# Giving the mixers of the second block instruction regions of their own

## The chip, the cores and the metric

The kernel runs on one core of a Trainium2 chip. The metric is device time in microseconds (us) of one execution. TensorE (PE) multiplies matrices, VectorE (DVE) and ScalarE (ACT) do element work, GpSimd (POOL) does some of it too, and SyncE (SP) starts transfers. Each engine runs its own list of instructions strictly in order; an instruction that waits for another engine holds up everything behind it in its list.

## The reference, cut to what matters

The program is a chain: a first transformer block with attention and a state-space part, a product-key expert layer ("Peer"), and a second block of two layers over 512 tokens of width 1024. A layer of the second block is

```
x = x + 0.5 * swiglu(rmsnorm(x, ffn1_norm), ffn1_gate, ffn1_up, ffn1_down)
z = rmsnorm(x, mix_norm) @ w_in
(aq, ak, av, iq, ik, iw, bq, bk, bv, bg, br, cu, dcq, dckv, dkpe) = split(z)
y_a = dsa_mixer(...)    # attention over the 256 or fewer keys that an index score picks
y_b = gla_mixer(...)    # gated linear attention in chunks of 64 tokens
y_c = conv_mixer(...)   # gate, 31-tap depthwise convolution, rmsnorm, silu
y_d = mla_mixer(...)    # latent attention with rope
x = x + concat([y_a, y_b, y_c, y_d]) @ w_out
x = x + 0.5 * swiglu(rmsnorm(x, ffn2_norm), ffn2_gate, ffn2_up, ffn2_down)
```

All of it is float32. The two layers have the same shapes.

## The kernel before, in words

The residual x stays in SBUF as hT: 8 chunks of 128 features by 512 tokens. Every large matrix product is taken as three matmuls (mm3, lines 209 to 211): weights and activations are split into a rounded high part and a low rest (wh, wl; xh, xl), and the products wh·xh, wh·xl and wl·xh are summed in PSUM. Weights arrive by SP transfers; `lw` copies the high part on ACT (line 1027) and subtracts it on DVE or POOL (line 1028).

The layer function (line 981) calls `ffn`, `mixer`, `ffn`. The `ffn` ends with 8 additions to hT on DVE (line 1067). Both begin with `scaled`, which makes xh on ACT (line 995) and xl on DVE (line 996) chunk by chunk, and with `rows_rstd` (squares on ACT at 1006, their sum on POOL at 1008).

The `mixer` writes its steps in an order laid down by hand (ORDER, line 830). The steps that matter here:

- "hp" and "conv" project the convolution's input (line 1558 is its first DVE instruction) and run 62 DVE instructions over 512 tokens (1571, 1573).
- "index" and "topk1" to "topk3" score keys and keep 256 of them: 16 rounds of a maximum and a replacement on DVE (1282, 1283), closed by line 1284, for 256, 384 and 512 columns.
- "mla0" to "mla3" are softmax blocks of the latent attention, 128 query rows and 4 heads each, over 128 to 512 keys: scores on PE (1432), scaled on ACT (1435) and on DVE (1436), then `softmax_pv`: maxima (DVE, 1220), exponentials (ACT, 1223), one half of the division on ACT and one on DVE (1230), transposes on PE (1233), copies (ACT, 1235) and products with the values (PE, 1240).
- "dsa0" to "dsa3" are the softmax blocks over the picked keys. They need the mask of their topk: bias and mask are added on DVE (1323, 1325), scores on PE (1328) are added to them on DVE (1329), then `softmax_pv`.
- "gla" and "conv_norm" need 1/sqrt of a mean square, taken as Ln (line 216) and Exp (217) on ACT; "silu" applies Silu on ACT (1150) to the gate tiles rg and the convolution's cv, and afterwards asks for the table of Ln and Exp again (1334). ACT holds one set of function tables at a time, and a change of set is an instruction of its own, ACT_TABLE_LOAD.
- "y4", "y2", "y6" split the results into high and low (194 on ACT, 195 on DVE).

Last comes the output projection "wo": 192 matmuls in two halves of 96 (WOP, YORD), the first over the parts of conv, gla and mla, the second over the rest, each added to hT on DVE (1212).

The text order is not the order of execution. A scheduler puts each engine's instructions into a list of its own. The first block stands in a `tc.block(name="first", schedule_with_timeline_sim=True)`; everything behind it, Peer, the four ffn and the two mixers, is one region, so an instruction of an ffn may stand between those of a mixer.

Of the kernel before, what the change touches and what calls it, by code (L numbers as in the profile page):

```python
# [919 lines left out]
class Block2:  # L920
# [60 lines left out]
    def layer(self, l, x):  # L981
        self.vec = self.vec2[:, l]
        self.ffn(l, 0, x)
        if l == 0:
            self.constants()
        self.mixer(l, x)
        self.ffn(l, 1, x)

    def scaled(self, x, g):
# [988 lines left out]
```

## Time and profile before

| what | us |
|---|---|
| runs, median (lowest to highest of 3) | 3770.8 (3761.55 to 3776.63) |
| the profiled execution | 3765.66 |
| its span, first to last instruction | 3763.8 |
| PE busy | 3593.1 (95% of the span) |
| DVE busy | 2592.4 (69%) |
| ACT busy | 1412.5 (38%) |
| POOL busy | 1087.1 (29%) |
| mean granted TensorE clock | 0.978 of full speed |

Busy shares are means over stages that differ, so the two mixers are looked at by themselves below. The profile shows them, in time from the span's start, at about 2028 to 2350 us and 3075 to 3400 us. Matmul ends are modelled: one 512-column mm3 matmul is shown as 0.39 us long, but starts follow one another closer than that.

### The profile page before, as it was taken

The numbers are of one execution on the slowest core, as the hardware profiler recorded it, in microseconds if no ns is written. First come the engines' busy times: TensorE is split into PE (matmuls) and PEld (weight loads), VectorE is DVE, ScalarE is ACT, GpSimd is POOL, SyncE is SP. The second block draws the span as 40 slices with busy tenths as digits, with TensorE's granted clock in tenths as the row PEclk, the third lists the DMA queues.
The fourth block names the chain that finished last, engine by engine and source line by source line (L and its number), as shares of the span: only waits on it lengthen the run. The fifth ranks groups of instructions, "written<-read, shape, count | busy, mean of one in ns | idle before, by whom it ended". The sixth has DMA issues, their size and how long they took to land. (4 is left out here: it accounts for less than half of the span.)

```text
span 3763.8 us, 46084 instructions
## 1 busy us (share of the span) xinstructions
PE 3593.1 (95%) x17229; PEld 2972.0 (79%) x17229; DVE 2592.4 (69%) x4504; ACT 1412.5 (38%) x2405; POOL 1087.1 (29%) x685
## 2 busy tenths in 40 slices
PE   7798979889999999999999899999999998999999
PEld 6656878878889988888887667888888875668887
DVE  9668999788888889854445987444444459975443
ACT  3253259423333333342223446322322234453222
POOL 4424767445555555530002222000100012210000
PEclk8899989999999999999999999999999999999999
DMA  4212225888888888833223111323332321112233
GB/s 119 78 40 94 76 91 224 284 304 295 286 307 292 301 291 297 301 111 95 93 98 94 64 46 56 96 95 95 96 95 95 98 93 54 46 45 95 95 96 101
DMA packets 181520, 529.88 MB, mean 141 GB/s; under 512 B 22256, under 2 KB 73008, under 8 KB 163120
## 3 DMA queue, kind: packets, MB, share of 16 engines
q1 hardware_dynamic: 157504, 388.64, 31.0%
q0 software_dynamic: 19392, 136.06, 9.8%
q10 hardware_dynamic: 4400, 2.24, 0.3%
q8 instruction: 136, 2.23, 0.2%
q14 instruction: 88, 0.72, 0.1%
HBM read 495.52 MB, written 30.18 MB: 140 GB/s over the span
## 5 line engine op out<-in xcount | busy, mean ns | idle before, releaser
L1027 ACT ACTIVATE wh<-wr 128x1024 fp32r<-128x1024 f32 (+1 forms) x334 | 347.4, 1040 | 1029.8 <-PE ps L210 766.0
L210 PE MATMUL ps<-x,wh 128*128 128x512 f32 x1408 | 548.8, 390 | 2.1 <-DVE x L996 2.0
L209 PE MATMUL ps<-x,wh 128*128 128x512 f32 x1408 | 549.1, 390 | 0.0
L211 PE MATMUL ps<-x,wl 128*128 128x512 f32 x1408 | 547.9, 389 | 0.0
L1028 DVE TENSOR_TENSOR wl<-wr,wh 128x1024 fp32r<-128x1024 f32 (+1 forms) x288 | 344.4, 1196 | 78.0 <-ACT wh L1027 71.1
L1008 POOL TENSOR_TENSOR s<-s,s 128x512 f32<-128x512 f32 x42 | 67.0, 1596 | 1125.2 <-ACT s L1006 1113.9
L1841 POOL TENSOR_TENSOR vl<-vr,vh 128x1024 fp32r<-128x1024 f32 x128 | 325.4, 2543 | 183.3 <-ACT vh L1840 178.2
L211 PE MATMUL S<-x,wl 128*128 128x384 f32 x1024 | 349.7, 341 | 8.1 <-POOL wl L1802 8.1
L209 PE MATMUL S<-x,wh 128*128 128x384 f32 x1024 | 349.4, 341 | 0.0
L210 PE MATMUL S<-x,wh 128*128 128x384 f32 x1024 | 348.6, 340 | 0.0
L1850 PE MATMUL V<-vl,ah 128*128 128x512 f32 x768 | 302.7, 394 | 12.0 <-POOL vl L1841 12.0
L210 PEld LDWEIGHTS ps<-x,wh 128*128 128x128 f32 x1408 | 264.3, 188 | 61.4 <-DVE x L996 5.9
L1850 PE MATMUL V<-vh,ah 128*128 128x512 f32 x768 | 300.7, 393 | 10.1 <-ACT vh L1840 10.1
L209 PEld LDWEIGHTS ps<-x,wh 128*128 128x128 f32 x1408 | 264.2, 188 | 55.8 <-issue 1.0
L211 PEld LDWEIGHTS ps<-x,wl 128*128 128x128 f32 x1408 | 264.3, 188 | 54.7
L1850 PE MATMUL V<-vh,al 128*128 128x512 f32 x768 | 302.5, 394 | 1.3 <-DVE al L195 1.3
L211 PE MATMUL ps<-ml,wl 128*128 128x512 f32 x704 | 278.1, 395 | 0.0
L209 PE MATMUL ps<-ml,wh 128*128 128x512 f32 x704 | 278.0, 395 | 0.0
L1914 POOL DMA_INDIRECT rows<-in_uv_dram,gidx x128 | 188.1, 1470 | 260.9 <-DVE acc L1923 230.9
L1055 DVE TENSOR_TENSOR s<-ps,rs 128x512 f32<-128x512 f32 x88 | 60.8, 691 | 278.8 <-PE ps L211 278.8
L1067 DVE SCALAR_TENSOR_TENSOR hT<-ps,hT 128x512 f32<-128x512 f32 x96 | 66.3, 691 | 270.7 <-PE ps L211 270.7
L1802 DVE TENSOR_TENSOR wl<-wr,wh 128x1024 fp32r<-128x1024 f32 x100 | 186.9, 1869 | 63.8 <-ACT wh L1800 63.7
(582 smaller groups left out, 7936.7 us busy)
## 6 DMA issues: line engine op xcount, KB each, us to landing
wr<-in_f_gu_dram SPq DMA_DIRECT2D x176, 512.0 KB, 3.7
wr<-in_ut_dram SPq DMA_DIRECT2D x128, 512.0 KB, 5.3
vr<-in_uv_dram SPq DMA_DIRECT2D x128, 512.0 KB, 4.8
wr<-in_f_dn_dram SPq DMA_DIRECT2D x64, 448.0 KB, 3.3
gates<-gst SPq DMA_DIRECT2D x12, 2048.0 KB, 6.8
gt<-gates SPq DMA_DIRECT2D x32, 768.0 KB, 7.3
wr<-in_w_dram SPq DMA_DIRECT2D x46, 512.0 KB, 3.4
wr<-in_f_dn_dram SPq DMA_DIRECT2D x32, 512.0 KB, 3.6
```

The lines of the kernel that those rows point to most:

```text
L209: mm(out, wh, xh, start=start, stop=False)
L210: mm(out, wh, xl, start=False, stop=False)
L211: mm(out, wl, xh, start=False, stop=stop)
L1008: nc.gpsimd.tensor_tensor(sq, acc, sq, op=OP.add)
L1027: nc.scalar.activation(hi, raw, AF.Copy)
L1028: (eng or nc.vector).tensor_tensor(lo, raw, hi.bitcast(F32), op=OP.subtract)
L1055: V.tensor_mul(u, ps[1], r)
L1067: V.scalar_tensor_tensor(x[:, m], ps, 0.5, x[:, m], op0=OP.mult, op1=OP.add)
L1802: e.tensor_tensor(ul, raw, uh.bitcast(F32), op=OP.subtract)
L1841: nc.gpsimd.tensor_tensor(vl, raw, vh.bitcast(F32), op=OP.subtract)
L1850: nc.tensor.matmul(ps[k], x[:, ts], y[:, cs], start=b == 0 and n == 0, stop=b == P - 1 and n == 2)
L1914: nc.gpsimd.indirect_dma_start(r, None, self.A["uv"], bass.IndirectOffsetOnAxis(ap=self.gi[:, s:s + 1], axis=0))
```

## The change

```diff
@@ Block2.layer
         if l == 0:
             self.constants()
-        self.mixer(l, x)
+        with self.tc.block(name=f"mixer{l}", schedule_with_timeline_sim=True):
+            self.mixer(l, x)
         self.ffn(l, 1, x)
```

Each mixer becomes a region of its own, and the scheduler weighs the order inside it by simulating a timeline. The instructions of the program are now: first block; Peer and the first ffn; mixer 0; two ffn; mixer 1; the last ffn. At an edge stands one branch per engine; no engine waits for another there, but no instruction crosses the edge. All lines behind 985 have a number higher by one in the changed kernel (1212 is 1213 there). On PE, DVE, POOL and SP the instructions are the same but for four branches each; on ACT there are also 14 more ACT_TABLE_LOAD, 7 in each mixer.

**ACT, mixer 0, near the last topk.** Before, the last rstd (convn) stands ahead of the Silu of the gate (rg), with one table load for all Silus:

```order
L242 ACTIVATE r_18788<-cv_17835 128x512
L216 ACTIVATE r_18791<-convn_18784,epsc 128x512
L217 ACTIVATE r_18791<-r_18791 128x512
L1223 ACTIVATE sm_18656,st_18676<-sm_18656,st_18676 128x384
L1223 ACTIVATE sm_18657,st_18676<-sm_18657,st_18676 128x384
L1223 ACTIVATE sm_18658,st_18676<-sm_18658,st_18676 128x384
L1223 ACTIVATE sm_18659,st_18676<-sm_18659,st_18676 128x384
L1150 ACT_TABLE_LOAD
L1150 ACTIVATE rg_18830<-rg_18830 128x512
```

Now, with the gate's Silu already done above these rows:

```order
L216 ACT_TABLE_LOAD
L216 ACTIVATE gl_18249<-gla_18245,epsc 128x512
L217 ACT_TABLE_LOAD
L217 ACTIVATE gl_18249<-gl_18249 128x512
L242 ACTIVATE gl_18272<-gla_18254 128x512
L1436 ACTIVATE sm_18378<-mla_18391,rqd_17795 128x128
L216 ACT_TABLE_LOAD
L216 ACTIVATE gl_18275<-gla_18271,epsc 128x512
L217 ACT_TABLE_LOAD
L217 ACTIVATE gl_18275<-gl_18275 128x512
```

The two rstd of gla (gl) and that of convn now come behind the gate's Silu; each loads a table for Ln and another for Exp, and cv's Silu loads a third kind again.

**DVE, mixer 0, at the end of the last topk** (ds is the index score; sm and sd hold softmax scores; the first row of either piece, 1284 before and 1285 now, closes topk3). Before:

```order
L1284 TENSOR_SCALAR ds_17342<-ds_17342 128x512
L1230 TENSOR_SCALAR sm_18657<-sm_18657,st_18676 128x384
L1230 TENSOR_SCALAR sm_18659<-sm_18659,st_18676 128x384
L1323 TENSOR_TENSOR sd_19060<-bias,ds_17342 128x256
L1325 TENSOR_SCALAR sd_19060<-ds_17342,b_16960 128x256
L1323 TENSOR_TENSOR sd_19061<-bias,ds_17342 128x256
```

Now, 13 rows behind that 1285 (between them stand the last splits of gl and dsa3's eight additions and two of its scores):

```order
L1437 SCALAR_TENSOR_TENSOR sm_18442<-mla_18446,rqd_17795,m_16956 128x128
L1221 TENSOR_REDUCE st_18462<-sm_18442 128x1
L1437 SCALAR_TENSOR_TENSOR sm_18443<-mla_18450,rqd_17795,m_16956 128x128
L1213 TENSOR_TENSOR hT<-hT,wo_19306 128x512
L1221 TENSOR_REDUCE st_18462<-sm_18443 128x1
L1213 TENSOR_TENSOR hT<-hT,wo_19320 128x512
L1330 SCALAR_TENSOR_TENSOR sd_19063<-dsa_19077,rq_18765,sd_19063 128x512
```

Before, the last row of an mla block's division (1230, of mla2) stands at the end of topk3. Now all of mla3 (sm_18442 and on) and then all of mla2 stand behind it, among the additions of wo's first half. On PE, the 96 matmuls of that first half stood among the dsa blocks before; now 89 of them stand ahead of mla3's transposes and 7 behind. The second half ended with 90 matmuls in a row before; now 24 of its matmuls stand at mla2 and the scores of dsa0, 12 at the end of dsa1 and dsa2, and 60 in a row behind all else.

**DVE, mixer 0, at its end.** Before, the last additions to hT alternate with the next ffn's xl (996) and its weights (1028):

```order
L1212 TENSOR_TENSOR hT<-hT,wo_19441 128x512
L996 SCALAR_TENSOR_TENSOR x_19591<-hT,vec_14586,x_19583 128x512
L1212 TENSOR_TENSOR hT<-hT,wo_19455 128x512
L1028 TENSOR_TENSOR wl_19505<-wr_19503,wh_19504 128x1024
L996 SCALAR_TENSOR_TENSOR x_19592<-hT,vec_14586,x_19584 128x512
L1212 TENSOR_TENSOR hT<-hT,wo_19475 128x512
```

Now:

```order
L1213 TENSOR_TENSOR hT<-hT,wo_19490 128x512
L1029 TENSOR_TENSOR wl_19506<-wr_19504,wh_19505 128x1024
L1029 TENSOR_TENSOR wl_19540<-wr_19538,wh_19539 128x1024
L1213 TENSOR_TENSOR hT<-hT,wo_19510 128x512
L1213 TENSOR_TENSOR hT<-hT,wo_19524 128x512
L1213 TENSOR_TENSOR hT<-hT,wo_19544 128x512
L1213 TENSOR_TENSOR hT<-hT,wo_19558 128x512
L986 UNCONDITIONAL_BRANCH
L997 SCALAR_TENSOR_TENSOR x_19592<-hT,vec_14586,x_19584 128x512
L997 SCALAR_TENSOR_TENSOR x_19593<-hT,vec_14586,x_19585 128x512
L997 SCALAR_TENSOR_TENSOR x_19594<-hT,vec_14586,x_19586 128x512
L1029 TENSOR_TENSOR wl_19574<-wr_19572,wh_19573 128x1024
```

The two weight tiles of wo's last four chunks (wl_19506, wl_19540) now stand behind the fourth of the last eight additions, and the next ffn's xl and its first weights (wl_19574) behind the eighth. At the entry the same holds: the mixer's eight 997 rows and its first weights stand behind all eight additions of the ffn.

## Rows read from the trace of the kernel before

**Rows 1.** Busy time of each engine by stretch: inside mixer 0, inside mixer 1, two ffn.

```profile
core 0: us, PE busy (x) PEld busy (x) DVE busy (x) ACT busy (x) POOL busy (x), PEclk, DMA share, GB/s
2070.00:2290.00 220.00, 200.54 (x965) 143.30 (x963) 205.25 (x440) 111.33 (x240) 52.02 (x28) 0.96 0.16 52
3110.00:3330.00 220.00, 196.61 (x929) 140.53 (x930) 206.68 (x431) 109.72 (x235) 50.03 (x21) 0.94 0.15 47
2420.00:3070.00 650.00, 650.00 (x2837) 532.16 (x2836) 284.58 (x335) 191.02 (x231) 19.70 (x12) 1.00 0.30 96
```

**Rows 2.** The same view, mixer 0: head to topk3's end, then three parts of the tail.

```profile
2042.00:2267.00 225.00, 203.41 (x962) 148.02 (x963) 208.14 (x419) 104.07 (x219) 56.16 (x30) 0.96 0.18 57
2267.00:2305.00 38.00, 36.29 (x191) 24.20 (x190) 33.26 (x73) 25.17 (x56) 9.90 (x5) 1.00 0.18 56
2305.00:2326.00 21.00, 21.00 (x117) 14.99 (x118) 13.00 (x31) 12.37 (x35) 0.00 (x0) 1.00 0.12 33
2326.00:2348.00 22.00, 22.00 (x98) 18.21 (x97) 16.90 (x18) 12.80 (x19) 8.62 (x6) 1.00 0.26 90
```

**Rows 3.** DVE's waits in mixer 0's head (us in total, times, longest).

```profile
DVE sm L1436 <- ACT sm L1435: 3.2, 4, 1.2
DVE tr L227 <- PE qkn L1297: 2.8, 1, 2.8
```

**Rows 4.** One line's instructions: topk3's closing DVE row, mixer 0 and 1.

```profile
L1284 DVE TENSOR_SCALAR ds<-ds x1: 428/428/428, 2267.1 to 2267.1; 128x512 f32<-128x512 f32 x1
...
L1284 DVE TENSOR_SCALAR ds<-ds x1: 420/420/420, 3313.7 to 3313.7; 128x512 f32<-128x512 f32 x1
```

**Rows 5.** The additions of wo to hT, mixer 0 and 1 (same view).

```profile
L1212 DVE TENSOR_TENSOR hT<-hT,wo x16: 672/679/689, 2287.3 to 2346.9; 128x512 f32<-128x512 f32 x16
...
L1212 DVE TENSOR_TENSOR hT<-hT,wo x16: 671/687/691, 3343.5 to 3396.9; 128x512 f32<-128x512 f32 x16
```

**Rows 6.** DVE's groups of the softmax blocks, mixer 0 (busy us, mean ns).

```profile
L1436 DVE SCALAR_TENSOR_TENSOR sm<-mla,rqd,m 128x128 f32<-128x128 f32 x16 | 5.3, 345 | 3.3 <-ACT sm L1435 3.2
L1220 DVE TENSOR_REDUCE st<-sm 128x1 f32<-128x512 f32 x4 | 2.5, 676 | 0.0
L1323 DVE TENSOR_TENSOR sd<-bias,ds 128x256 f32<-128x256 f32 x8 | 5.4, 689 | 0.5 <-PE dsa L1233 0.5
L1325 DVE TENSOR_SCALAR sd<-ds,b 128x256 f32<-128x256 f32 x4 | 2.2, 556 | 0.0
L1329 DVE SCALAR_TENSOR_TENSOR sd<-dsa,rq,sd 128x512 f32<-128x512 f32 x4 | 3.0, 738 | 0.0
```

**Rows 7.** ACT's groups, 2200 to 2348 us.

```profile
L1223 ACT ACTIVATE sd<-sd,st 128x512 f32<-128x512 f32 x4 | 2.9, 716 | 0.1
L1235 ACT ACTIVATE pt<-dsa 128x512 f32<-128x512 f32 x4 | 2.4, 597 | 2.4 <-PE dsa L1233 2.4
L1150 ACT ACT_TABLE_LOAD x1 | 1.3, 1283 | 0.0
```

**Rows 8.** Timeline at mixer 0's end: start, us, engine (ps: the next ffn's first product).

```profile
2345.76 0.39 PE L209 MATMUL ps<-x,wh 128*128 128x512 f32 x1
...
2347.45 0.74 DVE L996 SCALAR_TENSOR_TENSOR x<-hT,vec,x 128x512 fp32r<-128x512 f32 x1
...
2348.11 1.21 DVE L1028 TENSOR_TENSOR wl<-wr,wh 128x1024 fp32r<-128x1024 f32 x1
```

**Rows 9.** Timeline in mixer 0: PE idle in brackets, then two matmuls.

```profile
2178.45 1.12 PE L1115 MATMUL vtr<-cst,rg 128*128 128x128 f32 x4 [3.71 <-DVE rg L1086]
...
2180.65 0.63 PE L210 MATMUL win<-x,wh 128*128 128x512 f32 x1
2181.07 0.63 PE L211 MATMUL win<-x,wl 128*128 128x512 f32 x1
```

**Rows 10.** Busy time by stretch, as rows 1: PE's granted clock at two places.

```profile
2086.00:2097.00 11.00, 7.72 (x12) 2.83 (x11) 10.87 (x17) 6.52 (x16) 4.72 (x8) 0.53 0.35 105
...
2178.00:2182.00 4.00, 3.55 (x11) 2.94 (x12) 4.00 (x12) 1.18 (x3) 0.00 (x0) 0.57 0.33 113
```

## The prediction

> **What bounds the kernel now.** I read the stretches first. In the two ffn between the mixers PE is busy for the whole 650 us: 2837 matmuls, one every 0.229 us [rows 1]. A new order cannot shorten that, so only the mixers and their edges count. Inside them PE idles about 20 us in 220, while DVE is busy for 205 to 207 [rows 1]. Then I split mixer 0 at the end of its last topk, because the dsa blocks need the mask that topk3 makes. From the convolution's first DVE row to that point (2042 to 2267, "the head") DVE is busy for 208.1 of 225 us [rows 2]: the head is DVE's, with 16.9 us of idle, pieces of one to three microseconds behind ACT and PE [rows 3]. From there to the last addition into hT ("the tail") PE is busy for 36.3 of 38, 21.0 of 21 and 22.0 of 22 us [rows 2]: the tail is PE's, because wo's matmuls fill the time in which the softmax chains wait for DVE and ACT. It runs from 2267.1 to 2346.9 + 0.7 = 2347.6, or 80.5 us; in mixer 1 from 3313.7 to 3397.6, or 83.9 [rows 4, 5].
>
> **The change part by part.** The work is the same but for the table loads; what moves is order. All terms are for one mixer, in microseconds.
>
> *Tail: +11.5.* Before, mla3 and mla2 ran beside topk on DVE, and only the last transposes of mla2 were left when topk3 ended. Now both stand behind it, and I walk their chain with t = 0 at topk3's end:
> - DVE does two splits of 0.68, dsa3's additions 4 × (0.69 + 0.56), four scores of 0.74, mla3's 4 × (0.345 + 0.676) and three additions of wo of 0.68 [rows 5, 6]: 1.4 + 5.0 + 3.0 + 4.1 + 2.0 = 15.5. Then mla3's maxima are there.
> - PE has 89 matmuls of wo ahead of mla3's transposes, 89 × 0.229 = 20.4 [rows 1]. They start at about 2, and their list waits some 1.5 for DVE in between: t = 24. Two halves, each with transposes, two copies of 0.60 [rows 7], products and 7 wo in all, take about 6: t = 30.
> - mla2 starts there. Its scaling, maximum, four exponentials and division cannot overlap anything of its own; at three quarters of the 512-column durations they take 6.5, and the two halves with wo between them 6: t = 42.5.
> - dsa0 and dsa3 together: the remaining scores and maxima 5.5, exponentials 4 × 0.72 + 4 × 0.4 = 4.5, halves 5.5: t = 58. dsa1 and dsa2: DVE 8, exponentials 4.5, halves 6, less 1.5 that overlaps: t = 75. The 0.4 and the 8 are my estimates by width from rows 6 and 7.
> - 60 matmuls of wo, 60 × 0.229 = 13.7. Their last four chunks wait for weights that DVE now subtracts (1.21 [rows 8]) behind the fourth addition of wo: some 2.3. With the last addition: t = 92.
>
> So 92 against 80.5, where before 90 matmuls in a row could not start earlier because PE had been full; now PE idles in the chains. Bounds: if the chains hid entirely, PE's work alone, 192 × 0.229 = 44 plus the small matmuls of four blocks, some 17, would give 61 (-19). If wo's 60 all ran at the slow step below, 92 + 12 (+23.5).
>
> *Exit: +4.5.* Before, the next ffn's first matmul follows wo at once, at 2345.76, because its xl rows and weights alternate with wo's additions [rows 8]. Now they stand behind the eighth addition: wo's last matmul, then 1.1 to the end of that addition, three xl rows of 0.74, and the weights' subtraction of 1.21 [rows 8], without which the third matmul can't start: 1.1 + 2.2 + 1.2 = 4.5. Bounds 0 (if something still covers it) and 6.5 (a second pair of weights).
>
> *Entry: 0.* The same happens there: PE waits about 4 for xl and weights. But the next bound is DVE, which waits for the row norm; its chain of squares and sums keeps its place, and the projections' matmuls were waiting for it before. Bounds 0 to +3.
>
> *Table loads: +3.* 7 × 1.283 = 9.0 on ACT [rows 7], all near topk3's end, where the two splits of cv stand ahead of topk3's last DVE row and wait for cv's Silu. About 20 of DVE's own topk work lies beside these loads, so most is hidden; 0 to 9, and I take a third. The Trainium skill, "ScalarE: Activation LUTs", section "Table sets: the hidden batching unit", says to group activation calls by set, not by function, and this order breaks its rule: Silu is pulled ahead of two Ln/Exp pairs, then comes back. Its price of about 2.7 us for a switch would make it 18.9 on ACT and the sum some 14 higher for both mixers; the row has 1.283 for the load itself, and I go by the row.
>
> *Head: -6.* With each instruction at the usual duration of its group, the DVE list up to topk3's end sums to 186.7 now and to 189.7 in the old order (rows 2 have 208.1 for the old one, since some rows took longer than usual): the work that moved behind it (mla3, mla2) and the work that moved ahead (gate products, splits) nearly cancel, -3. Of the 16.9 of DVE idle [rows 2] the new order may close some or none: it mixes topk with the other chains earlier. No row tells how much; bounds -16 and 0; as each of the pieces has a chain on ACT or PE behind it [rows 3] that the new order does not shorten, I take -3.
>
> *Sum:* 11.5 + 4.5 + 0 + 3 - 6 = +13 for a mixer, +26 for both. The two mixers have the same pieces, and mixer 1's stretches look alike [rows 1], so I don't treat it apart. The profiled execution took 3765.7 us, so 3791.7 by its own time; it lies 5.1 below the median of the three runs, so against that median I expect 3797.
>
> **The rivals.**
>
> *The clock falls in the tail (slower still).* After an idle of 3.71 us PE's matmuls follow one another at 0.42 to 0.43 us instead of 0.229 [rows 9, 1], and the granted clock is 0.57 there, 0.53 in an earlier stretch of 11 us [rows 10]: the lower level, 1.2 GHz. The new tail has some 30 us in which PE has only short work between waits. If one such stretch of 11 us falls into each of the two dsa stages or the wo behind them, it costs up to 5 each: +10 for a mixer, 3797 + 20 = 3817. The Trainium skill, "TensorE: Matmul & The Clock Gate", Part 1, says that the low clock is the default and that activity releases it; rows 10 fit that. Against this rival: in the tail before, the clock was 1.00, and in the new one wo's 89 and 60 run unbroken.
>
> *The idle closes (faster).* DVE's order is the one thing that the head hangs on. If nearly all of the 16.9 goes, the head gains 3 + 16 = 19, and if ACT's loads stay hidden and the exit costs 4.5, the tail decides: with mla2 overlapping mla3's halves and dsa's additions it may come down to 82, +1.5. Then -13 for a mixer: 3771 - 26 = 3745. It decides where the head's gain exceeds what tail and exit cost, 6 in this case and 16 by my walk. For it speaks that DVE's idle is in many short pieces; against it, that two whole softmax chains stand alone behind topk3.
>
> *Order moves the idle about (no change).* Head -12, tail +8, exit +4: 3771. For it: PE and DVE work are unchanged, and each is over 90% busy in the head.
>
> That the change does nothing is excluded by the order of the instructions.
>
> **How the numbers follow.** I give my forecast 0.45, its own range 3780 to 3815; the falling clock 0.14; no change 0.25; faster 0.16. About 0.5% (19 us) is what a measurement of this kernel can tell from no change: below 3752 is faster, above 3790 slower. Of the forecast three quarters lie above 3790: slower 0.34 + 0.14 + 0.02 from the edge of "no change" = 0.50. Same: 0.11 + 0.23 = 0.34. Faster: 0.16. The range leaves out a tenth at each side: it goes down to 3747, into the faster case, and up to 3828, past the falling clock. Likeliest is the forecast, 3797.
>
> **What would show it.** Right: topk3's end at the same distance behind the convolution's first row, 219 to 228 us; the time from there to the last addition of wo 88 to 96 instead of 80.5; PE idle of several microseconds in that tail, which had almost none; a PE gap of 3 to 6 us between the mixer's last wo matmul and the ffn's first; seven more table loads in each mixer, 1.28 each; the ffn stretches unchanged. Wrong: a tail of 80 or less, which would mean that the chains overlap better than I walked them; a head of under 215, which would mean that the idle was order alone; a Peer or ffn stretch whose length changes, since nothing moves there but at the edges; a clock under 0.9 in the tail, which is the first rival.

## The result and the profile after

The changed kernel takes **3882.3 us** (median of four runs, 3880.22 to 3889.28), against 3772.0 for the kernel before beside it (3761.55 to 3776.63): 1.03 times as long, 95% interval 1.0274 to 1.0325. Slower was right; the size, +110 us, is four times the forecast's +26 and lies outside the range.

The profiled execution took 3889.28 us, 7.0 above its median, and that of before lies 6.4 below its own, so the traces show 123.6 where the medians show 110.3. The page of after, its line of busy times:

```profile
PE 3648.7 (94%) x17229; PEld 3005.6 (77%) x17229; DVE 2611.6 (67%) x4504; ACT 1431.3 (37%) x2419; POOL 1096.9 (28%) x685
```

ACT has 14 instructions more, the table loads. PE is busy 55.6 us longer with the same work; the mean granted clock is 0.961 instead of 0.978.

Where the time went is found by cutting each mixer at five instructions that both traces have: the last addition of the ffn (1067, now 1068), the convolution's first DVE row (1558/1559), topk3's closing row (1284/1285), the last addition of wo (1212/1213), and the next ffn's first product row on DVE. In us, mixer 0 / mixer 1:

| stretch | before | after | difference |
|---|---|---|---|
| entry | 12.9 / 12.4 | 21.3 / 17.7 | +8.4 / +5.3 |
| head | 225.2 / 227.6 | 230.9 / 228.1 | +5.7 / +0.5 |
| tail | 80.0 / 83.5 | 122.8 / 119.2 | **+42.8 / +35.7** |
| exit | 12.1 / 12.1 | 23.2 / 23.2 | +11.1 / +11.1 |
| sum | 330.3 / 335.6 | 398.2 / 388.2 | +67.9 / +52.6 |

The sums give 120.5 of the 123.7 by which the spans differ; the stretches of ffn alone are unchanged. The rest lies ahead of the first ffn (3.4), where the program is the same: over the traces of all runs here that point is reached between 1657.0 and 1665.8 us. So a single execution's whole time says less than its stretches. Two thirds of the 120.5 lie in the tail. Busy times of after, mixer 0: the head; then the tail, cut at the ends of the divisions of mla2, of dsa0 and dsa3, of dsa1 and dsa2, and at the last addition; then the exit (columns as in [rows 1]):

```profile
2053.90:2284.80 230.90, 203.70 (x913) 150.12 (x913) 218.60 (x404) 107.96 (x202) 62.01 (x30) 0.93 0.19 60
2284.80:2329.60 44.80, 38.99 (x169) 27.00 (x167) 23.86 (x48) 18.77 (x39) 4.75 (x2) 0.88 0.15 48
2329.60:2350.10 20.50, 15.19 (x69) 11.22 (x70) 8.64 (x27) 9.30 (x27) 0.00 (x0) 0.83 0.00 1
2350.10:2377.90 27.80, 20.39 (x78) 12.53 (x79) 14.29 (x40) 10.68 (x33) 0.00 (x0) 0.62 0.00 0
2377.90:2407.60 29.70, 28.23 (x132) 21.22 (x131) 8.71 (x16) 9.55 (x21) 0.00 (x0) 0.85 0.11 36
2407.60:2430.80 23.20, 16.86 (x58) 12.07 (x59) 17.27 (x13) 14.18 (x21) 11.71 (x7) 0.85 0.20 69
```

The same three late steps of the tail before (dsa0 and dsa3, where the last of mla2 lies too; dsa1 and dsa2; wo's rest):

```profile
2267.50:2298.50 31.00, 29.56 (x142) 18.97 (x141) 29.29 (x63) 22.56 (x51) 9.90 (x5) 1.00 0.17 52
2298.50:2317.00 18.50, 18.23 (x107) 13.24 (x106) 12.55 (x34) 9.07 (x28) 0.00 (x0) 1.00 0.10 29
2317.00:2347.50 30.50, 30.50 (x155) 24.35 (x154) 20.32 (x25) 17.77 (x30) 8.62 (x6) 1.00 0.27 88
```

The dsa steps together take 48.3 now and 49.5 before, the rest 29.7 and 30.5. So the late steps did not stretch: 44.8 us, in which mla3 and mla2 are worked off (and, beside them, dsa3's additions and scores and wo's first half), stand ahead of steps that are as long as before. In the dsa steps no engine is full now: PE 35.6 of 48.3 us, DVE 22.9, ACT 20.0. PE's four longest waits from topk3's end to the last addition (us in total, times, longest):

```profile
PE mla L1234 <- ACT sm L1231: 5.2, 1, 5.2
PE dsa L1234 <- ACT sm L1231: 4.8, 1, 4.8
PE dsa L1234 <- ACT sd L1231: 4.4, 1, 4.4
PE dsa L1329 <- DVE sd L1330: 2.0, 1, 2.0
```

Each of the first three is a softmax chain's division that PE's transposes wait for. The granted clock of the second dsa step is 0.62, so for most of it PE had the lower level (1.2 GHz, which would read 0.5); the same step had 1.00 before.

At the exit PE waits for the next ffn's first operands, which before cost 0.2 us (one wait, for an xl row, 996). After, 2407.6 to 2431:

```profile
PE ps L209 <- ACT wh L1028: 3.2, 1, 3.2
PE ps L211 <- DVE wl L1029: 2.0, 1, 2.0
PE ps L210 <- DVE x L997: 1.9, 3, 0.7
```

At the entry the same happens, and DVE's first convolution row comes late. The timeline of after (last value: idle before the row, and what ended it):

```profile
2031.88 0.69 DVE L1068 SCALAR_TENSOR_TENSOR hT<-ps,hT 128x512 f32<-128x512 f32 x1 [4.21 <-PE ps L211]
...
2033.56 7.73 POOL L1009 TENSOR_TENSOR s<-s,s 128x512 f32<-128x512 f32 x4 [3.15 <-ACT s L1007]
...
2033.98 2.29 DVE L1029 TENSOR_TENSOR wl<-wr,wh 128x1024 fp32r<-128x1024 f32 x1
2036.19 1.76 DVE L997 SCALAR_TENSOR_TENSOR x<-hT,vec,x 128x512 fp32r<-128x512 f32 x1
...
2053.90 0.69 DVE L1559 TENSOR_TENSOR hp<-win,rs 128x512 f32<-128x512 f32 x1 [9.03 <-PE win L211]
```

Beside POOL's four additions of squares one xl row takes 1.76 us here and a weight's subtraction 2.29, where [rows 8] has 0.74 and 1.21; most of the eight xl rows (median 0.746) take no longer than there.

### The profile page after: what moved, and what is told of

Read it like the earlier page. It is cut to its first block, busy times and chain, and to the rows that moved or that the text cites. A ratio compares the mean times of both kernels' runs of the same rounds, so it can differ in the third digit from the quotient of the medians.

```text
span 3887.5 us, 46082 instructions
## 1 busy us (share of the span) xinstructions
PE 3648.7 (94%) x17229; PEld 3005.6 (77%) x17229; DVE 2611.6 (67%) x4504; ACT 1431.3 (37%) x2419; POOL 1096.9 (28%) x685
## 3 DMA queue, kind: packets, MB, share of 16 engines
q8 instruction: 136, 2.23, 0.2%
## 5 line engine op out<-in xcount | busy, mean ns | idle before, releaser
L210 PEld LDWEIGHTS ps<-x,wh 128*128 128x128 f32 x1408 | 265.1, 188 | 67.0 <-DVE x L997 11.5
L1851 PE MATMUL V<-vh,ah 128*128 128x512 f32 x768 | 302.1, 394 | 12.3 <-ACT vh L1841 12.3
L1915 POOL DMA_INDIRECT rows<-in_uv_dram,gidx x128 | 189.8, 1483 | 259.2 <-DVE acc L1924 234.5
L1803 DVE TENSOR_TENSOR wl<-wr,wh 128x1024 fp32r<-128x1024 f32 x100 | 178.6, 1786 | 72.8 <-ACT wh L1801 72.6
```

Of the source, the lines that this page charges most:

```text
L210: mm(out, wh, xl, start=False, stop=False)
L1803: e.tensor_tensor(ul, raw, uh.bitcast(F32), op=OP.subtract)
L1851: nc.tensor.matmul(ps[k], x[:, ts], y[:, cs], start=b == 0 and n == 0, stop=b == P - 1 and n == 2)
L1915: nc.gpsimd.indirect_dma_start(r, None, self.A["uv"], bass.IndirectOffsetOnAxis(ap=self.gi[:, s:s + 1], axis=0))
```

## The experiments

The theory after the result: the simulated order makes the tail longer, because it lets topk overtake mla3 and mla2; the edges cost their own part; table loads and the clock come on top. The rivals: the edges alone (all that may not cross them) make all of it; or the softmax chains cost the same wherever they stand, so that putting them back ahead of topk gains nothing. The cuts of code show the lines that matter; those that only set up names for them are left out.

### Edges without the simulated order

```diff
-        with self.tc.block(name=f"mixer{l}", schedule_with_timeline_sim=True):
+        with self.tc.block(name=f"mixer{l}"):
```

> The regions stay, but the order inside them is not weighed by a simulated timeline: edges alone. The changed kernel's trace puts the loss of some 121 us in four places: entry +8.4 and +5.3, head +5.7 and +0.5, tail +42.8 and +35.7, exit +11.1 and +11.1 (mixer 0, mixer 1). Theory 'inner order': the tail is what the simulated order costs, so this kernel loses only the edges, 36 us or less: 3785 to 3810, tail 80 to 84 as before. Rival 'edges': cutting the ffn off from the mixer starves PE and the rest follows from that: 3850 or more, tail over 100.

It took 3813.1 us, 1.0114 times as long as before (1.0095 to 1.0134): +41. The head is 230.8 / 227.7, the tail 79.4 / 82.6 as before, the entry 23.7 / 23.3 and the exit 23.2 / 23.2. Tail and exit, mixer 0:

```profile
2282.50:2361.90 79.40, 77.42 (x394) 55.49 (x392) 54.32 (x113) 41.44 (x96) 10.50 (x4) 1.00 0.17 54
2361.90:2385.10 23.20, 16.94 (x58) 11.98 (x59) 17.28 (x13) 14.18 (x21) 11.71 (x7) 0.85 0.20 69
```

The rival that the edges make all of it falls: with them alone the tail keeps length and clock. They do cost about 41 us by themselves, 5 above what was expected; the other 69 of 110 come with the simulated order.

### One region around the whole second block

Both layers stand in one timeline region, with no edge inside. One edge is left, between Peer and the first ffn, where the kernel before has none.

```diff
+    with tc.block(name="second", schedule_with_timeline_sim=True):
         for l in range(2):
             b2.layer(l, hT)
```

> The whole second block is one region with a simulated order: no edge at any mixer. Theory 'edges and order add': the edges-only run lost 41 us, so this one loses 110 - 41 = 69: 3835 to 3850, with entry 13, head and tail as in the changed kernel, exit 12 to 13. Rival 'the edges' price is hidden once the tail is long': 3865 or more.

3858.35 us, 1.0214 (1.0197 to 1.0231): +83.5, between the two forecasts. The entry, 13.5 / 12.5, is back near the old value and the exit, 9.9 / 9.9, under it; the tail is 127.0 / 119.4:

```profile
2280.70:2407.70 127.00, 106.81 (x462) 75.23 (x459) 65.23 (x136) 56.34 (x129) 14.88 (x9) 0.83 0.09 30
2407.70:2417.60 9.90, 9.73 (x41) 7.18 (x40) 5.92 (x5) 6.03 (x8) 1.51 (x1) 1.00 0.29 100
```

The long tail needs no edge at a mixer. 41 + 83.5 is 14 more than the 110 of both together. Two terms of about that size stand in the traces. The entry makes 8: it is 21.3 / 17.7 with edges and simulated order, 23.7 / 23.3 with edges alone. And the first ffn, from Peer's last addition to its own, takes 377.0 us here and 366.9 before, 10 that the table of the mixers does not hold. At its start PE waits for the first weights, as at the exit of a mixer; PE's longest wait there, this run, then before:

```profile
PE ps L209 <- ACT wh L1027: 4.1, 3, 3.4
```

```profile
PE ps L210 <- DVE x L996: 1.6, 6, 0.3
```

So of the 83.5 about 10 come with the edge that this edit sets at Peer's end, though the ffn's own order is a simulated one here as well. The rest, some 73, is still more than the 41 of the edges alone.

### Mixer and the following ffn in one region

```diff
         with self.tc.block(name=f"mixer{l}", schedule_with_timeline_sim=True):
             self.mixer(l, x)
-        self.ffn(l, 1, x)
+            self.ffn(l, 1, x)
```

> The changed kernel with the ffn behind each mixer taken into the mixer's region: the edge at the mixer's exit is gone, the one at its entry stays. Theory 'the exit's price is the edge': from the last addition of wo to the ffn's first DVE product 12 to 15 us instead of 23.2, so 16 to 22 us less than the changed kernel: 3860 to 3867. Rival 'the exit's price is the simulated order' (60 matmuls of wo behind everything, xl behind all additions): 23 stays, 3878 to 3886.

3870.22 us (3864.5 to 3880.65), 1.0261 (1.0244 to 1.0279). The exit went from 23.2 to 9.9 / 10.0, better than expected, and PE's only wait there is 0.2 us; the tail stayed at 122.2 / 121.0. The median is 95 above the kernel before beside it, where the change is 110 above; by the stage table mixer 0 gained 15.4 and mixer 1 12.5. The edge has moved rather than gone: it now stands between the two ffn behind mixer 0. From the first one's last addition to the second one's first product, this run, then after:

```profile
2760.00:2781.40 21.40, 15.79 (x57) 11.43 (x58) 15.24 (x14) 10.36 (x16) 9.92 (x6) 0.92 0.21 74
```

```profile
2781.70:2794.30 12.60, 12.60 (x56) 10.06 (x55) 4.42 (x6) 6.21 (x9) 1.88 (x2) 1.00 0.25 83
```

The two ffn together take 724.0 us instead of 714.4, so 9.6 of the 27.9 is lost again. Behind mixer 1 no ffn follows the one in the region, so nothing is paid there.

### The additions of the squares moved from POOL to DVE

On the edges-only kernel, in the ffn behind each mixer:

```diff
-                nc.gpsimd.tensor_tensor(sq, acc, sq, op=OP.add)
+                (eng or nc.gpsimd).tensor_tensor(sq, acc, sq, op=OP.add)
...
-                    r = self.rows_rstd(x)
+                    r = self.rows_rstd(x, eng=V if i else None)
```

> The edges-only kernel, with the seven additions of the squares for the ffn behind each mixer moved from POOL to DVE (line 1009, 42 becomes 14 fewer on POOL). In the edges-only kernel the eight xl rows behind the exit take 1.76 us each (median) while POOL adds squares, against a shortest of 0.74. Theory 'POOL slows DVE': the xl rows come back to 0.74 to 0.8 us, and the eight of them with what stands between end earlier or no later than 13 us behind the last addition of wo, although DVE does 7 x 0.7 more. Rival 'they wait for xh': the median stays over 1.5 us.

One execution took 3804.2 us, beside 3773.0 for the kernel before (4.3 of its gain on the kernel with edges lies ahead of the first ffn, where nothing changed). The exit is 19.5 / 20.0 instead of 23.2, and the eight xl rows end 10.6 us behind wo's last addition, within the 13 that the theory expected. The xl rows (count; shortest, median, longest ns) in the kernel with edges, then in this one:

```profile
L997 DVE SCALAR_TENSOR_TENSOR x<-hT,vec,x x8: 736/1763/1771, 2361.8 to 2374.9; 128x512 fp32r<-128x512 f32 x8
```

```profile
L997 DVE SCALAR_TENSOR_TENSOR x<-hT,vec,x x8: 743/745/747, 2357.4 to 2367.3; 128x512 fp32r<-128x512 f32 x8
```

The same rows take 1.76 us while POOL adds squares and 0.745 when it doesn't. The exit's 3.7 / 3.2 is about half of what I mis-sized there; the wait for wh on ACT (3.2 us) is in both.

### mla's blocks put back ahead of topk3

`behind(late, early)` sets an order on one engine, with no wait. topk3's first round comes behind mla1's division, its ninth behind mla3's, its closing row behind mla2's.

```diff
-        for _ in range(16):
-            V.max(m8, acc)
+        for k in range(16):
+            mx = V.max(m8, acc)
+            if k in after:
+                self.behind(mx, [self.divs[after[k]]])
...
+        if 16 in after:
+            self.behind(last, [self.divs[after[16]]])
```

> The changed kernel, with topk3 held back on DVE: its first round stands behind mla1's division, its ninth behind mla3's, its close behind mla2's. Theory 'mla behind topk': the tail loses the 55 us that mla3 and mla2 take there in the changed kernel and falls to about 70; DVE gets some of it back as idle in the head, 10 to 25 for a mixer; in all 30 to 60 us faster than the changed kernel, 3825 to 3855. Rival 'the chains cost the same wherever they stand': head longer by what the tail is shorter, 3870 to 3890.

3870.65 us, 1.0263 (1.0243 to 1.0283). The tail is 81.2 / 76.8, as short as before: the walk was right on what lengthened it (wo's first half went ahead of topk3's end with the chains). But the head is 268.9 / 266.9, 38 longer:

```profile
2049.70:2318.60 268.90, 239.24 (x1076) 176.46 (x1075) 232.93 (x439) 129.10 (x243) 68.58 (x32) 0.93 0.18 60
```

DVE stands idle for 36.0 us in it, against 12.3 in after; the other 14 of the 38 are rows that moved in with the chains. The rival is right on the total: in this order, the two chains cost about 40 us per mixer at either place. Before, both stand in a head of 225.2 us in which DVE idles for 16.6, and of that only 4.6 is for ACT's steps of the mla blocks. In that order their rows alternate with topk's rounds on DVE over a long stretch, while the hold puts topk3's rounds behind whole chains. That the alternation is what saves the time fits this; no run here set it alone.

### No extra table loads

The Silus are held behind the Exps of gla and convn, so that the loads fall back to the old number.

```diff
-                self.tc.keep_in_program_order(nc.scalar.activation(t, t, AF.Silu))
+                self.behind(self.tc.keep_in_program_order(nc.scalar.activation(t, t, AF.Silu)), v["exps"])
```

> The changed kernel, with the gate's and the convolution's Silu held behind the three Exp of gla and convn on ACT: the 14 extra table loads are gone (34 as before, not 48), the rest of the order nearly the same. Theory 'loads on the path': in the trace the chain to topk3's end runs through them (DVE waits 2.06 and 2.23 us there, and mla1's exponentials stand behind four of them), so 5 to 9 us for a mixer come back: 3864 to 3874. Rival 'loads hidden': 3879 to 3886.

3874.37 us, 1.0272 (1.0252 to 1.0293): about 8 less than after, 0.6 for each of the 14 loads, 0.4 above the range that was expected if they are on the path and 4.6 below the rival's. The head is 3.3 / 5.8 shorter, the tail much the same (123.1 / 121.1). The change's loads are 1.28 us each, and some of them end DVE's waits: ACT, then DVE, around convn's rstd (r) and the split of cv in after:

```profile
2271.99 1.28 ACT L216 ACT_TABLE_LOAD   x1
2273.29 0.69 ACT L216 ACTIVATE r<-convn,epsc 128x512 f32<-128x512 f32 x1
2273.99 1.28 ACT L217 ACT_TABLE_LOAD   x1
2275.29 0.63 ACT L217 ACTIVATE r<-r 128x512 f32<-128x512 f32 x1
...
2277.92 1.28 ACT L1151 ACT_TABLE_LOAD   x1
```

```profile
2275.95 1.42 DVE L1581 SCALAR_TENSOR_TENSOR cv<-cv,vec,r 128x512 f32<-128x512 f32 x2 [2.06 <-ACT r L217]
...
2282.50 0.69 DVE L195 TENSOR_TENSOR x<-cv,x 128x512 fp32r<-128x512 f32 x1 [2.23 <-ACT x L194]
```

The load, cv's Silu and its rounding follow r, and DVE stands for 2.06 and 2.23 us while topk3's rounds are queued behind the waiting row.

### Both, and wo held behind mla2

Both edits together:

> The changed kernel with both: topk3 held behind the mla blocks, and the Silus behind the Exps. If the two causes add: the gain of the run with topk3 held back plus that of the run without the loads, 3810 to 3845. If the loads only hurt because mla stood behind them, the sum is smaller than that by what the loads gave alone.

3860.39 us, 1.0241 (1.0221 to 1.0262); the range was missed. Head 259.2 / 263.2, tail 75.7 / 77.0. The two gains do add, though: 11.6 for the order held back and 7.9 for the loads make 19.5, and this run is 21.9 below after. What was wrong is the size that I had given the order's gain.

Then after with wo's first half held behind mla2's last product on PE, to see whether its 89 matmuls delay the two chains:

```diff
                         net.mm3(ps, (wh[:, m - m0, k - a], wl[:, m - m0, k - a]), (yh[c], yl[c]), k == a, k == e - 1)
+                        if k == a:
+                            self.behind(net.mm, [v["pv"]])
```

> The changed kernel with wo's matmuls held behind mla2's last product on PE, so that wo's first half no longer stands ahead of mla3's transposes but fills the waits of the dsa blocks, as before the change. Theory 'wo stands in the way': mla3 and mla2 take 25 us of the tail instead of 45, the dsa blocks and wo 79 as now, since there wo runs in their waits; tail 100 to 108, in all 30 to 45 us faster than the changed kernel, 3837 to 3852. Rival 'chains alone': PE's place of wo doesn't matter, because DVE and ACT set the pace; 3875 to 3885.

3872.88 us, 1.0263 (1.0245 to 1.028), 2 under the rival's range and far from the theory's. The tail is 115.8 / 115.6. mla3 and mla2 are done after 32.4 instead of 44.8, but what follows takes 83.4 instead of 78.0:

```profile
2276.80:2309.20 32.40, 19.80 (x69) 9.75 (x68) 15.90 (x39) 14.82 (x35) 0.00 (x0) 0.66 0.00 1
2309.20:2392.60 83.40, 75.54 (x372) 56.47 (x372) 41.43 (x92) 33.23 (x83) 4.79 (x2) 0.91 0.12 38
```

The two chains, with PE free for them, need 32 us here, at a granted clock of 0.66. wo's matmuls then have to be done later.

All three holds:

> The changed kernel with all three holds: Silus behind Exps, topk3 behind the mla blocks, wo behind mla2. If wo's matmuls ahead of mla3's transposes are what keeps the head long in the run with the first two holds (259 and 263 us), the head falls to 240 to 250 and the tail rises from 76 to 80 to 84: 3840 to 3855. If the mla chain itself is as long in any place, the head stays at 255 to 262 and the whole at 3860 to 3872.

3858.89 us, 1.022 (1.0203 to 1.0237): between the two forecasts, 1 below the rival's range and 4 above the other. Head 251.3 / 247.9, tail 85.3 / 85.3, so this run decides for neither. And these three in one region for the whole second block, the best that I could make of the simulated order:

> One region for the whole second block with a simulated order and the same three holds: no edges. If edges and order add, 40 to 44 us less than the run with the three holds and regions for each mixer: 3797 to 3815, still slower than the kernel before. Rival: with the order mended, the simulated timeline's better exit (9.9 us instead of 12.1) shows, and it is within 10 us of the kernel before.

3835.91 us, 1.0159 (1.0142 to 1.0176). Missed by 21: entry and exit are repaired (13.5 / 12.5, 9.9), but head and tail stay at 253.4 / 247.4 and 89.8 / 89.8, and the first ffn, behind this region's own edge, takes 376.3 us instead of 366.9, which neither forecast had. The tail:

```profile
2303.90:2393.70 89.80, 81.75 (x395) 59.95 (x394) 56.27 (x110) 40.75 (x95) 15.15 (x9) 0.93 0.12 42
```

It is 46 faster than the change and 1.6% slower than the kernel before. No version of the whole program that I ran beats the kernel before.

### PE kept busy in the waits

Needless transposes, 256 in all, ahead of the dsa blocks' own transposes:

```diff
                 tp = net.ps()
+                for k in range(16 if c == 0 and fill else 0):
+                    nc.tensor.transpose(tp[:, :P], ident, ident)
```

> The changed kernel with 16 needless transposes of the identity ahead of each of the first two transposes groups of every dsa block (32 a block, overwritten at once by what they stand ahead of): they run while PE waits for the exponentials there. Theory 'the clock': granted clock in the dsa blocks back from 0.67 to 0.74 to over 0.95, and the stretch from mla2's end to the last addition of wo shorter than 78 us by 5 to 10 although PE does some 15 us more. Rival 'clock of no matter': that stretch the same or longer.

One execution took 3883.9 us. The stretch from mla2's division to the last addition went from 78.0 to 71.2 us in mixer 0 and from 74.5 to 70.5 in mixer 1, although PE has more to do there. Its three parts, mixer 0:

```profile
2331.20:2351.40 20.20, 18.81 (x108) 14.75 (x109) 8.94 (x27) 9.51 (x27) 0.00 (x0) 0.90 0.00 1
2351.40:2375.40 24.00, 21.20 (x140) 15.79 (x139) 13.71 (x39) 10.39 (x34) 0.00 (x0) 0.93 0.00 1
2375.40:2402.40 27.00, 24.71 (x128) 18.14 (x126) 8.71 (x15) 9.37 (x21) 0.00 (x0) 1.00 0.12 40
```

The clock is 0.90, 0.93 and 1.00 instead of 0.83, 0.62 and 0.85, in the dsa steps a little under the expected 0.95. So in this one execution the fallen clock costs the dsa steps and wo at least 4 to 7 us per mixer, a ninth to a sixth of the tail's growth. The part with mla3 and mla2 in front, which has no such transposes, was 2.4 and 3.2 us longer here, and the whole time shows no gain.

### The kernel before without half of wo

```diff
-WOP = ((0, 4, 2), (4, 8, 2))
+WOP = ((4, 8, 2),)
```

> The kernel before, with the first half of wo left out (96 of 192 matmuls and 8 of 16 additions in each mixer; its weights are not loaded either), everything else in its place. In the kernel before, PE is busy for 79 of the 80 us of the tail. Theory 'the chains set the pace': wo only fills their waits, so the dsa divisions stay where they were (dsa0 and dsa3 at 23 to 31, dsa1 and dsa2 at 45 to 50 us behind topk3's end) and the tail falls by less than 12 us of the 22 that are left out. Rival 'PE sets the pace', as my prediction read it: the divisions come 10 to 20 us earlier and the tail falls to 58 to 62.

One execution took 3761.8 us, beside 3777.8. 96 matmuls in each mixer, 22 us at 0.229 [rows 1], are gone, and mixer 0's tail is 79.5 us against 80.0 (mixer 1: 73.1 against 83.5). Its windows, and the ends of the divisions, first this kernel and then before (count; shortest, median, longest ns; first and last start):

```profile
2269.70:2299.00 29.30, 24.49 (x103) 15.05 (x101) 23.55 (x60) 19.86 (x48) 0.15 (x1) 0.86 0.11 37
2299.00:2322.90 23.90, 18.13 (x78) 11.71 (x78) 11.29 (x30) 9.90 (x29) 0.00 (x0) 0.67 0.00 1
2322.90:2349.10 26.20, 25.89 (x133) 20.89 (x133) 18.20 (x21) 15.98 (x27) 9.67 (x6) 1.00 0.18 61
```

```profile
L1230 DVE TENSOR_SCALAR sd<-sd,st x4: 347/414/478, 2298.0 to 2317.7; 128x512 f32<-128x512 f32 x2, 128x256 f32<-128x256 f32 x2
```

```profile
L1230 DVE TENSOR_SCALAR sd<-sd,st x4: 348/414/2562, 2295.6 to 2312.7; 128x512 f32<-128x512 f32 x2, 128x256 f32<-128x256 f32 x2
```

From topk3's end (2269.7 here, 2267.5 before) the first and last of these rows start at 28.3 and 48.0 us here, at 28.1 and 45.2 before. With 22 us of PE work less, mixer 0's divisions stand nearly where they stood: the chains set the pace there, and wo's matmuls had filled their waits. Three things limit this. In mixer 1 the same rows start at 25.1 and 39.9 us here, at 30.6 and 46.3 before, and the tail gained 10 us of the 22, so PE's work is not without weight; the 58 to 62 of the rival is far from either. With PE emptier its clock fell to 0.86 and 0.67, which works against the gain: by the 4 to 7 us of the run with needless transposes, PE's share could be up to about 7 us in mixer 0 and 17 in mixer 1 (an estimate). And both heads are 5 to 6 us longer here, with a wait of DVE of 5 us for ACT at the index scores that the kernel before does not have; why was not tried.

## Why the prediction was right in sign and wrong in size

**"The tail is PE's" is the step that failed.** I read PE's 36.3 of 38, 21.0 of 21 and 22.0 of 22 us [rows 2] as a bound, and so expected that two chains more in the tail could run beside the rest: dsa0 to dsa3 in 15.5 + 17 us behind mla2. From division to division they took 20.5 + 27.8, about the 49.5 of before. PE had been full because wo's matmuls were put into the chains' waits (the run without half of wo: nearly so in mixer 0, in part in mixer 1). Seen so, a chain that stands alone is paid in full, and 44.8 us for mla3 and mla2 ahead of an unchanged rest is what the table shows. Only the last step is PE's own, matmuls of wo in a row: 30.5 of 30.5 us before, and there the forecast of 17 came out as 15.2.

**The walk, point by point** (t from topk3's end, mixer 0; forecast, then measured): mla3's maxima 15.5, 19.5; mla2 begins 30, 36.9; mla2 done 42.5, 55; dsa0 and dsa3 58, 84; dsa1 and dsa2 75, 107.6; last addition 92, 122.8. The order of the steps is right. Each is later, and most so in the dsa steps, to the end of their products 29 and 23.6 us where I had 15.5 and 17: there I summed busy times, with little for the waits between engines. The parts ahead of mla2 were 7 us short and its own 5.6.

**The clock.** The rival was right in direction: the tail's stretches have 0.88, 0.83, 0.62 and 0.85 where I argued that wo's runs would hold 1.00. I gave it 0.14 and 10 us a mixer; the filler shows at least 4 to 7. It came with the waits and adds to them. The Trainium skill, "TensorE: Matmul & The Clock Gate", Part 1, says that the throttled clock is the default and activity releases it. Here the trace agrees: needless transposes in the waits raised 0.62 to 0.93.

**Exit: +11.1, not +4.5.** The place was right: xl and weights behind the eighth addition, and PE waits for them. I took xl at 0.74 us, but beside POOL's additions of squares it takes 1.76, and I left out the first wh on ACT, 3.2 of wait. The Trainium skill, "SBUF — State Buffer", section "SBUF: two separate sides", has VectorE and GpSimd exclude each other at a shared port pair when a DVE instruction reads two SBUF inputs and GpSimd reads SBUF too; here the xl rows fell to 0.745 us once POOL's additions were gone, as that says. Other rows are looked at under the head, below.

**Entry: +8.4 / +5.3, not 0.** I said that DVE would not feel it because it waits for the row norm. In fact its first convolution row waited 9.03 us for PE's projection, and PE had waited 2.4 us for a weight and 1.4 for an xl row. Without the edge the entry is back at 13.5 / 12.5 (one region).

**Table loads: +3.** Right: 3.3 and 5.8 in the heads, some 8 us in all. The load itself is 1.28 us, as in [rows 7]. My side remark of some 14 more at the dearer price does not follow from my own third: a third of 18.9 - 9.0 is 3.3 for a mixer, 6.6 for both.

**Head: -6.** Wrong: +5.7 / +0.5, of which the loads make 3.3 / 5.8. DVE's idle closed by little: 12.3 of 230.9 us against 16.9 of 225, but its busy time is 218.6 where [rows 2] has 208.1. The stretches have slightly different bounds. The work did shrink, by 4.0 us at each row's shortest duration, as forecast (-3), but single rows take longer. Against the shortest row of the same line, tiles and shape, 16 DVE rows of mixer 0's head take over 0.3 us more before and 21 after, 27.0 and 39.5 us more in all (mixer 1: 30.9 and 38.2). Each of these rows overlaps a subtraction of weights on POOL (1028, now 1029). The convolution's rows, before, then after:

```profile
L1573 DVE SCALAR_TENSOR_TENSOR cv<-hp,dw,cv x60: 732/739/2879, 2047.4 to 2123.0; 128x512 f32<-128x512 f32 x60
```

```profile
L1574 DVE SCALAR_TENSOR_TENSOR cv<-hp,dw,cv x60: 737/748/3444, 2059.5 to 2134.6; 128x512 f32<-128x512 f32 x60
```

I had seen that some rows took longer (208.1 against 189.7) and took their time as given; the new order raised it. No run took POOL's subtractions out of the heads. Nor is the head's growth of mixer 0 all the new order's: with edges alone it was 230.8 as well, there as idle of DVE.

**The sum.** Per mixer, forecast and measured in mixer 0: tail +11.5, +42.8; exit +4.5, +11.1; entry 0, +8.4; table loads and head -3, +5.7. What I named against the fast rival, two whole softmax chains alone behind topk3, is what happened; it was priced as overlap. None of the signs named as "wrong" came true but the clock under 0.9.

## What to carry to other kernels

An engine that is busy all through a stretch need not bound it: ask whether its work is a chain or filler in the waits of one, and price a moved chain at its latency, with its waits, not at its busy time. A cut between two regions costs what had been done across it, here 5 to 11 us at each place, even though nothing waits at the cut; moving the cut moves the cost. And where a hand-made interleaving keeps several chains going at once, putting one of them somewhere else in a worse order moves much of its latency along: three holds took 37.5 and 33.9 us from the two tails and put 20 of them into each head.

## What I had not expected of the hardware

- A DVE row with two SBUF inputs (xl) went from 0.745 to 1.76 us while POOL added tiles of the same size (128x512). A weight's subtraction (128x1024) took 2.29 us at the entry against 1.21 in [rows 8]; both such rows lie inside POOL's four additions, but a run without them was not made.
- In the heads every DVE row that took over 0.3 us more than its kind overlaps a POOL subtraction, up to 3.44 us for a convolution row of 0.74.
- The granted clock fell to 0.62 over the 27.8 us of the second dsa step, whose matmuls had 1.00 before with wo's between them, and 256 needless transposes brought 0.93 back; the step took 24.0 us with them.
